# First layer's normalisation moved behind its input projection: x arrives transposed, the per-token root is applied to the products

## Chip, cores and metric

One core of a Trainium2 chip runs the whole program. The metric is the device time of one execution in microseconds (us), the median of the runs; lower is better. All tensors are float32. A matrix product in float32 is made of three passes: each operand is split into a high part in the format fp32r and a low part (what the high part leaves over), and high x high, high x low and low x high are summed in PSUM.

## What is computed

The reference is a trunk of two layers over 512 tokens and 1024 features. Cut to what the change touches:

```python
def rms_norm(x, g):
    xf = x.astype(jnp.float32)
    y = xf * lax.rsqrt(jnp.mean(xf * xf, axis=-1, keepdims=True) + NORM_EPS)
    return (y * g.astype(jnp.float32)).astype(x.dtype)

def hybrid_layer(x, w_in, w_out, g_pre, g_post, lb, g_head, sinks):
    h = rms_norm(x, g_pre)
    proj = jnp.einsum('bsd,de->bse', h, w_in)
    q_h, f_h, i_h, z_h, q_a, k_a, v_a, z_a = jnp.split(proj, SPLIT_POINTS, axis=-1)
    o_h = rms_norm(hgrn2(q_h, f_h, i_h, lb), g_head).reshape(B, S, HG_WIDTH) * jax.nn.silu(z_h)
    o_a = sliding_window_attention(rotary(q_a), rotary(k_a), v_a, sinks) * jax.nn.silu(z_a)
    y = jnp.einsum('bse,ed->bsd', jnp.concatenate([o_h, o_a], axis=-1), w_out)
    return x + rms_norm(y, g_post)
```

The root of a token (the rsqrt) is one number for a row of h. Since the projection is linear, it may be multiplied into h before the projection or into the row of proj after it. The weight g_pre belongs to a feature.

## The kernel before

**Tiling.** P = 128 partitions; the 512 tokens are NT = 4 tiles, the 1024 features KT = 8 tiles. hT (hhi and hlo, L421) holds the normalised input transposed, feature on partition: 8 feature tiles by 512 tokens. The input projection is cut into a narrow piece "kv" (keys and values, 256 columns) and 12 slabs of 512 columns: QA (attention queries, 2 slabs), IV (i, 2), FQ (forget logits and q of HGRN2, 4), ZA and ZH (the gates, 2 each). The order of the slabs is the list ORDER (L128); "kv" is first, QA second. A slab is four units of 8 steps, and a step is three matmuls of 128x512 (L293). Two units run interleaved, with three PSUM banks "pj" to take turns. For slabs with the feature on the partition (QA, FQ, ZA) the weight is the stationary operand and hT streams; for IV, ZH and kv the tokens are on the partition.

**Weights.** A weight piece (128x512) is loaded by SyncE's queue (SP) into one of 4 buffers "raw", cast to its high part whi by ScalarE (ACT, L181), and the low part wlo is made by VectorE (DVE), for odd pieces of QA by GpSimd (POOL) (L182). A load into raw waits until the piece four before it has been split. The pieces of kv are called wkv (L1013, L1014). Attention and recurrence are emitted between the steps (L968 to L975). A helper `later` runs a function after so many steps; `pin` keeps an instruction in program order on its engine, while the others are ordered by the scheduler when the program is built.

**The start (L981 to L1057).** x is loaded token by token, in tiles of 128x512 called a and x (L978), and gcol, the weight g_pre of layer 0 as 128x8, on ACT's queue. TensorE (PE) turns gcol into two banks of rows (gpre, L1005). For each token tile: ACT squares x and sums it (L383, L386), POOL takes the power -0.5 (L354, L393), DVE multiplies x by root and weight (xn, L401), PE transposes in eight pieces into PSUM (L406), ACT casts to hhi (L410) and DVE makes hlo (L414). Token tiles 1 to 3 are emitted as halves between the steps of kv. kv itself is four units, one for each token tile (24 matmuls of 128x256 each), whose result ACT copies into rkv (L448). Then comes slab QA; its results are multiplied by the tables cos_f and sin_f (tile cs) on DVE (L504 to L511). Constants are loaded and prepared during the first steps of QA.

**Results that the change touches.** IV is copied by ACT (L651). FQ: ACT takes sigmoid of a logit and of its negative from PSUM (L665, L666), or silu of q (L674). ZA: ACT takes silu from PSUM (L845), DVE multiplies by the attention output (L846). ZH: ACT takes silu (L859).

## Time and profile before

| what | value |
|---|---|
| median of 3 runs | 922.8 us (922.64 to 923.39) |
| span of the profiled execution, first to last instruction | 921.4 us |
| around the span (median less span) | 1.4 us |
| busy PE / DVE / ACT / POOL in it | 904.5 / 667.3 / 463.4 / 272.9 us |
| first matmul of slab QA in it | at 24.48 us |

A row of a timeline is: start, duration, engine, line, operation, output <- input, shape, how many merged, and in brackets the idle time of the engine before it with what ended it. "SPq" and "ACTq" are DMA issues in the queues of SyncE and ScalarE. A busy row says how long the engine was occupied in a stretch; the granted clock stands in the column PEclk (1.00 is full speed).

### The profile page before, as it was taken

The page shows a single profiled execution, that of the slowest core. Times are in us where ns is not written, and L with a number is a line of the kernel's source. Part 1 is how long each engine was busy: PE and PEld are TensorE (multiplying, and loading weights), DVE is VectorE, ACT ScalarE, POOL GpSimd, SP SyncE. Part 2 cuts the span into 40 slices and gives each one's busy share as a digit, 9 for nine tenths or more (in the row PEclk, how much of TensorE's full clock was granted, in tenths as well). Part 3 has the DMA queues.
Part 4 walks back from the last instruction along what each step waited for, and adds up shares of the span by engine and source line. Part 5 has one row for each costly group of instructions (what it writes and reads, how often), then busy time and mean ns, then how long its engine had stood idle before and what let it go on. Part 6 is the DMA issues. An engine that isn't in the chain of part 4 may idle for free.

```text
span 921.4 us, 19000 instructions
## 1 busy us (share of the span) xinstructions
PE 904.5 (98%) x7240; PEld 752.0 (82%) x7240; DVE 667.3 (72%) x1326; ACT 463.4 (50%) x1100; POOL 272.9 (30%) x292
## 2 busy tenths in 40 slices
...
GB/s 224 192 231 136 172 36 81 92 93 94 70 85 54 130 91 70 92 106 129 111 164 177 161 147 173 58 69 92 94 70 81 96 77 94 82 47 94 136 35 137
DMA packets 56570, 100.74 MB, mean 109 GB/s; under 512 B 6560, under 2 KB 9120, under 8 KB 56480
## 3 DMA queue, kind: packets, MB, share of 16 engines
...
q14 instruction: 33, 0.27, 0.1%
q10 hardware_dynamic: 288, 0.14, 0.1%
...
## 4 chain that ended last, share of the span: by engine, by line
PE 88%; DVE 6%; ACT 3%; issue 1%; POOL 1%; DMA 0%; POOLq 0%; DVEq 0%; ACTq 0%
PE pj L293 72%; PE sc L561 2%; PE sc L744 2%; PE ac L614 2%; PE ac L815 2%; DVE wlo L182 1%; PE ac L818 1%; PE ac L802 1%; PE sc L588 1%; ACT s L575 1%; PE sc L867 1%; PE sc L790 1%; POOL r L354 1%; DVE a L943 1%; PE sc L550 0%
## 5 line engine op out<-in xcount | busy, mean ns | idle before, releaser
L182 DVE TENSOR_TENSOR wlo<-raw,whi 128x512 fp32r<-128x512 f32 x249 | 182.9, 748 | 50.0 <-ACT whi L181 49.3
L181 ACT CAST whi<-raw 128x512 fp32r<-128x512 f32 x256 | 154.2, 620 | 106.0 <-PE pj L293 95.2
L293 PE MATMUL pj<-hhi,wlo 128*128 128x512 f32 x512 | 203.8, 398 | 0.0
L293 PE MATMUL pj<-hhi,whi 128*128 128x512 f32 x512 | 199.8, 390 | 0.0
L293 PE MATMUL pj<-hlo,whi 128*128 128x512 f32 x512 | 199.6, 390 | 0.0
L293 PE MATMUL pj<-whi,ops 128*128 128x512 f32 (+1 forms) x520 | 172.5, 394 | 0.0
L293 PEld LDWEIGHTS pj<-hhi,whi 128*128 128x128 f32 x512 | 96.1, 188 | 20.7
L293 PEld LDWEIGHTS pj<-whi,ops 128*128 128x128 f32 x520 | 97.2, 188 | 19.3
L293 PEld LDWEIGHTS pj<-hhi,wlo 128*128 128x128 f32 x512 | 96.1, 188 | 19.3
L293 PEld LDWEIGHTS pj<-hlo,whi 128*128 128x128 f32 x512 | 96.3, 188 | 18.6
L293 PE MATMUL pj<-whi,hlo 128*128 128x512 f32 x256 | 103.6, 405 | 0.0
L293 PE MATMUL pj<-wlo,ops 128*128 128x512 f32 (+1 forms) x260 | 100.8, 388 | 0.0
L293 PE MATMUL pj<-wlo,hhi 128*128 128x512 f32 x256 | 100.5, 392 | 0.3 <-DVE wlo L182 0.2
L293 PE MATMUL pj<-whi,hhi 128*128 128x512 f32 x256 | 100.3, 392 | 0.0
L763 POOL TENSOR_TENSOR k<-k,tot 128x256 f32<-128x256 f32 x80 | 64.2, 831 | 107.2 <-PE sc L744 57.7
L575 ACT ACTIVATE s<-sc,negm 128x128 f32<-128x128 f32 x128 | 45.5, 368 | 38.9 <-DVE negm L569 34.8
L762 DVE TENSOR_TENSOR q<-q,tot 128x256 f32<-128x256 f32 x80 | 48.8, 647 | 12.8 <-PE sc L750 7.0
L293 PEld LDWEIGHTS pj<-whi,hhi 128*128 128x128 f32 x256 | 48.1, 188 | 10.3
L293 PEld LDWEIGHTS pj<-wlo,ops 128*128 128x128 f32 x260 | 49.0, 188 | 8.8
L293 PEld LDWEIGHTS pj<-wlo,hhi 128*128 128x128 f32 x256 | 48.3, 189 | 9.1 <-DVE wlo L182 1.2
L293 PEld LDWEIGHTS pj<-whi,hlo 128*128 128x128 f32 x256 | 48.2, 188 | 8.0
L582 POOL TENSOR_TENSOR s<-s,sums 128x512 f32<-128x512 f32 x32 | 34.1, 1067 | 44.5 <-DVE sums L580 29.2
...
## 6 DMA issues: line engine op xcount, KB each, us to landing
...
```

What stands on the lines that cost most here:

```text
L181: keep(nc.scalar.copy(hi, v))
L182: keep((nc.gpsimd if i in on_pool and i % 2 else nc.vector).tensor_tensor(lo, v, hi.bitcast(F32), op=ALU.subtract))
L293: nc.tensor.matmul(u.o, lhsT=u.sta(k, u.w)[i], rhs=u.mov(k, u.w)[j], start=(n == 0), stop=(n == len(u.list) - 1))
L354: keep(nc.gpsimd.tensor_tensor(r, t, mhalf[:, 0:1], op=ALU.pow))
L561: pin(nc.tensor.matmul(S[:, h * 256:(h + 1) * 256], lhsT=q[:, 2 * hp_ + h, t_], rhs=kst[v][p][:, (n - 1) * P:(n + 1) * P], start=(h == 0 a ...
L575: nc.scalar.activation(pt[:, h * P:(h + 1) * P], cur[h], AF.Exp, bias=negm[:, h:h + 1], scale=SCALE, accum_out=sums[:, h:h + 1])
L582: nc.gpsimd.tensor_tensor(pv, pv, sums.unsqueeze(2).broadcast_to([P, 4, P]), op=ALU.mult)
L614: pin(nc.tensor.matmul(U, lhsT=vst[v][:, blk, :], rhs=d, start=(i == 0), stop=(i == len(terms) - 1)))
L744: pin(nc.tensor.matmul(L[32 * b:32 * b + 32, c:c + 16], lhsT=k[:, o_:o_ + 32], rhs=qv[:, blk:blk + qu, 1, :], start=True, stop=True, tile_ ...
L762: nc.vector.tensor_tensor(qv[:, :, 1, :], qv[:, :, 1, :], tv[:, :, 0].unsqueeze(2).broadcast_to([P, nb, hh]), op=ALU.mult)
L763: nc.gpsimd.tensor_tensor(kv_[:, :, 0, :], kv_[:, :, 0, :], tv[:, :, 1].unsqueeze(2).broadcast_to([P, nb, hh]), op=ALU.mult)
L815: pin(nc.tensor.matmul(O[:, c], lhsT=A[:, c], rhs=vs(j, n), start=(n == 0), stop=False))
```

## The change

A new input xt is x transposed on the host. Layer 0 no longer normalises and transposes:

- Eight feature tiles xs (128 features x 512 tokens) are loaded in the order in which they are needed, each pair followed by its kv weight. The first kv weight goes on ACT's queue ahead of gcol.
- hhi and hlo are x times g_pre, without the root: ACT multiplies by gcol with the cast (`high`), DVE multiplies and subtracts (`low`). The squares go another way: those of feature tiles 0, 1, 4, 5 are made elementwise on POOL, of 2, 3, 6, 7 on ACT, added up on DVE (seven adds), and summed over the partitions by four matmuls with a column of ones (total). DVE and POOL make rcol from it, the root with the token on the partition (128x4).
- The products of kv run feature tile by feature tile over all four token tiles, in two banks; the first low part of kv's weights is DVE's, the other three are POOL's.
- After two steps of QA, PE transposes rcol into a row (four transposes, rrow 128x512). The tables of QA are multiplied by it, one on DVE, one on POOL. FQ and ZA of layer 0 get one more DVE multiplication each by rrow (16 and 8 instructions of 128x512), from PSUM. kv, IV and ZH take rcol as the scale of the ACT instruction that they had.
- Constants are prepared from step 4 of QA, as before; the load of the masks waits for the four matmuls of total, whose ones lie in its buffer.

Layer 1 is not touched. The removed parts are two broadcasts of gcol and 32 transposes on PE, the scale and hlo of L401 and L414 on DVE, the squares and casts of L383, L386 and L410 on ACT, and five of POOL's small instructions.

DVE at the start of the program, before: the rows from the first root to the first two low parts of QA's weights (sc are PSUM tiles with the transposes, gcol's rows lie in PSUM as ac).

```order
L401 SCALAR_TENSOR_TENSOR xn<-a,r_140,ac_82 128x512
L401 SCALAR_TENSOR_TENSOR xn<-a,r_140,ac_81 128x512
L414 TENSOR_TENSOR hlo<-sc_79,hhi 128x4x128
L1013 CAST wkv<-raw 128x512
L414 TENSOR_TENSOR hlo<-sc_80,hhi 128x4x128
L1013 CAST wkv<-raw 128x512
L1014 TENSOR_TENSOR wkv<-raw,wkv 128x512
```

The same engine and place in the changed kernel, from the first weight cast to the first low part of QA's weights (a and b are the squares).

```order
L1032 CAST wkv<-raw 128x512
L1027 SCALAR_TENSOR_TENSOR hlo<-xs,gcol,hhi 128x512
L1035 TENSOR_TENSOR wkv<-raw,wkv 128x512
L1027 SCALAR_TENSOR_TENSOR hlo<-xs,gcol,hhi 128x512 x5
L1070 TENSOR_TENSOR a<-a 128x512 x2
L1027 SCALAR_TENSOR_TENSOR hlo<-xs,gcol,hhi 128x512 x2
L1073 TENSOR_TENSOR a<-a,b 128x512 x2
L1074 TENSOR_TENSOR a<-a 128x512
L1076 TENSOR_TENSOR a<-a,b 128x512 x2
L182 TENSOR_TENSOR wlo<-raw,whi 128x512
L1087 TENSOR_SCALAR t<-sc_79 128x4
```

All inputs of the new rows up to L182 lie in SBUF; of the old ones most have an input in PSUM. The low part of QA's first weight now stands behind all adds.

POOL at the same place, before and then in the changed kernel.

```order
L354 TENSOR_TENSOR r_140<-s_138,mhalf 128x1
L1014 TENSOR_TENSOR wkv<-raw,wkv 128x512 x2
L391 TENSOR_SCALAR s_172<-ss 128x1
L393 TENSOR_TENSOR r_174<-s_172,mhalf 128x1
L1014 TENSOR_TENSOR wkv<-raw,wkv 128x512
L354 TENSOR_TENSOR r_183<-s_181,mhalf 128x1
L391 TENSOR_SCALAR s_238<-ss 128x1
L393 TENSOR_TENSOR r_240<-s_238,mhalf 128x1
L182 TENSOR_TENSOR wlo<-raw,whi 128x512 x4
```

```order
L1054 TENSOR_TENSOR a<-xs 128x512 x2
L1035 TENSOR_TENSOR wkv<-raw,wkv 128x512 x2
L1065 TENSOR_TENSOR b<-xs 128x512 x2
L1035 TENSOR_TENSOR wkv<-raw,wkv 128x512
L182 TENSOR_TENSOR wlo<-raw,whi 128x512
L1089 TENSOR_TENSOR rcol<-t,mhalf 128x4
L182 TENSOR_TENSOR wlo<-raw,whi 128x512 x2
L1102 TENSOR_TENSOR cs<-cs,rrow 128x512
```

Up to the second large row of QA's weights POOL now has eight instructions of 128x512 in a row, six of them on x and its products; before it had three, with small ones between, and four on QA's weights later.

PE where kv ends and QA begins, changed kernel (rows of three, a step, are alike).

```order
L1041 MATMUL pj<-wkv,hhi 128x256 x4
L1083 MATMUL sc_79<-u,a 128x2 x4
L293 MATMUL pj<-hhi,wlo 128x512
L293 MATMUL pj<-hlo,whi 128x512
L293 MATMUL pj<-hhi,whi 128x512
L293 MATMUL pj<-hhi,wlo 128x512
L293 MATMUL pj<-hlo,whi 128x512
L293 MATMUL pj<-hhi,whi 128x512
L1099 MATMUL sc_80<-ident,rcol 128x128 x4
```

Behind this place PE's order is that of before, but for the transposes of the keys, which come three steps later.

The diff, cut to its core:

```diff
+        def load_tables():
+            rot.append(big.tile([P, 2, 512], F32, tag="q", name="cs", bufs=QB))
+            nc.sync.dma_start(rot[0][:, 0], cos_f)
+            nc.sync.dma_start(rot[0][:, 1], sin_f)
...
-            nc.scalar.copy(rkv[0][:, tt], o)
+            if l:
+                nc.scalar.copy(rkv[0][:, tt], o)
+            else:
+                nc.scalar.activation(rkv[0][:, tt], o, AF.Copy, scale=rcol[:, tt:tt + 1])
...
+                    if not l:
+                        nc.vector.tensor_tensor(f, o, rrow, op=ALU.mult)
+                        o = f
+                    nc.scalar.activation(k, o, AF.Sigmoid, scale=-1.0)
                     nc.scalar.activation(f, o, AF.Sigmoid)
-                    nc.scalar.activation(k, o, AF.Sigmoid, scale=-1.0)
...
+                    if not l:
+                        nc.vector.tensor_tensor(qT[h], o, rrow, op=ALU.mult)
+                        o = qT[h]
                     nc.scalar.activation(qT[h], o, AF.Silu)
...
+                if not l:
+                    nc.vector.tensor_tensor(z, o, rrow, op=ALU.mult)
+                    o = z
                 nc.scalar.activation(z, o, AF.Silu)
...
+    raws[0] = wp.tile([P, 512], F32, tag="raw", name="raw", bufs=RAW_BUFS)
+    nc.scalar.dma_start(raws[0].rearrange("p (a c) -> p a c", a=2), pieces[0])
     nc.scalar.dma_start(gcol, gcol_c)
+    state["raw"] = 1
+    for k in range(KT):
+        load_x(k)
+        if k % 2:
+            w_load(k // 2 + 2)
...
+    def first_kv(load_tables, rot, kv_evac):
+
+        warm = pj()
+        for n in (512, 256):
+            pin(nc.tensor.matmul(warm[:, 0:n], lhsT=ones[:, 0:P], rhs=ones[:, 0:n], start=True, stop=True))
+        A, V, G = nc.scalar.copy, nc.vector.tensor_tensor, nc.gpsimd.tensor_tensor
...
+        high(0)
+        whigh(0, C)
+        low(0)
+        high(1)
+        wlow(0, V)
+        low(1)
+        prod(0, ((0, 0), (1, 0), (0, 1)))
+        for c in range(2):
+            pin(G(sq[0][c], xk(c), xk(c), op=ALU.mult))
+        prod(1, ((0, 0), (1, 0), (0, 1)))
+        for j in range(1, KT // 2):
+            high(2 * j)
+            whigh(j, A)
+            low(2 * j)
+            wlow(j, G)
+            high(2 * j + 1)
+            low(2 * j + 1)
+            for c in range(2):
+                if j == 2:
+                    pin(G(sq[j][c], xk(2 * j + c), xk(2 * j + c), op=ALU.mult))
+                else:
+                    pin(nc.scalar.activation(sq[j][c], xk(2 * j + c), AF.Square))
...
+            prod(2 * j, ((0, 0), (1, 0), (0, 1)))
+            prod(2 * j + 1, ((0, 0), (1, 0), (0, 1)))
+            w_load(min(KT // 2 + j, KT // 2 + RAW_BUFS - 1))
+        load_tables()
+        total = sc()
+        for tt in range(NT):
+            pin(nc.tensor.matmul(total[:, 2 * tt:2 * tt + 2], lhsT=sq[0][0][:, tt * P:(tt + 1) * P], rhs=ones[:, 0:2], start=True, stop=True))
...
+        pin(nc.gpsimd.tensor_tensor(rcol, t, mhalf, op=ALU.pow))
...
+        def row():
+            bank = sc()
+            for tt in range(NT):
+                pin(nc.tensor.transpose(bank[:, tt * P:(tt + 1) * P], rcol[:, tt:tt + 1].broadcast_to([P, P]), ident))
+            pin(nc.scalar.copy(rrow, bank))
+            nc.vector.tensor_tensor(rot[0][:, 0], rot[0][:, 0], rrow, op=ALU.mult)
+            nc.gpsimd.tensor_tensor(rot[0][:, 1], rot[0][:, 1], rrow, op=ALU.mult)
+
+        later(2, None, row)
+        later(3, None, evacs)
+        later(4, None, constants)
```

155 lines of the change are left out of this document (64 added, 91 removed).

## The prediction

> **What bounds the kernel now.** I read the page's busy times first, then the stages, then the timeline of the start.
>
> ```profile
> PE 904.5 (98%) x7240; PEld 752.0 (82%) x7240; DVE 667.3 (72%) x1326; ACT 463.4 (50%) x1100; POOL 272.9 (30%) x292
> ```
>
> PE is busy for 98%: 17 us of the span are all that it lacks, so only PE work taken away or PE idle time filled can pay. Where is it idle at the start? A row is a stretch, its length, and PE, PEld, DVE, ACT and POOL busy.
>
> ```profile
> 0.00:5.00 5.00, 3.33 (x8) 1.78 (x9) 0.60 (x3) 2.93 (x6) 0.68 (x6) 1.00 0.56 173
> 5.00:10.00 5.00, 4.76 (x26) 3.28 (x25) 3.21 (x7) 3.36 (x6) 3.16 (x4) 1.00 1.03 354
> 10.00:15.00 5.00, 4.12 (x32) 3.65 (x31) 3.60 (x8) 3.60 (x8) 2.60 (x4) 1.00 1.00 330
> 15.00:20.00 5.00, 5.00 (x45) 4.95 (x44) 4.00 (x7) 1.75 (x5) 0.79 (x2) 1.00 0.56 175
> 25.00:30.00 5.00, 5.00 (x24) 4.13 (x23) 4.92 (x8) 2.83 (x7) 2.46 (x2) 1.00 0.67 209
> ```
>
> From 15 us on PE has no gap. The change rewrites what lies before slab QA, so its gain or loss is how much sooner or later QA's first matmul starts, plus PE work that moves behind it. Now:
>
> ```profile
> 21.51 2.18 PE L293 MATMUL pj<-wkv,hhi 128*128 128x256 f32 x16
> 23.52 1.12 PE L293 MATMUL pj<-wkv,hlo 128*128 128x256 f32 x8
> 24.48 0.40 PE L293 MATMUL pj<-hhi,wlo 128*128 128x512 f32 x1
> ```
>
> QA starts at 24.48. Matmuls of 256 columns run at 0.12 us each ((23.52 - 21.51) / 16 = 0.126, (24.48 - 23.52) / 8 = 0.12), so kv's 96 cost PE 11.5 us; the rest of the 24 us are 40 transposes, the warm-up matmuls and gaps.
>
> **The new start: first PE and ACT alone.** The 32 transposes of x and 8 of gcol go. Rows of the chain of waits price four at:
>
> ```profile
> 15.88 0.44 PE sc L406 x4
> ```
>
> 32 of them are 3.5 us. The products of kv are the same 96. ACT has 15 large instructions (8 highs, 3 casts, 4 squares); four such casts merged take 2.18 us, so 0.53 each and 8 us in all:
>
> ```profile
> 21.83 2.18 ACT L181 CAST whi<-raw 128x512 fp32r<-128x512 f32 x4
> ```
>
> The first data:
>
> ```profile
> 0.78 0.40 ACTq L981 DMA_DIRECT2D gcol<-in_gcol_dram  x1
> 3.47 0.63 ACT L386 ACTIVATE hlo<-a 128x512 fp32r<-128x512 f32 x1 [0.75 <-DMA a<-in_x_dram]
> 5.97 1.32 ACT L1013 CAST wkv<-raw 128x512 fp32r<-128x512 f32 x2 [1.06 <-DMA raw<-in_wkv_dram]
> 10.39 0.63 ACT L386 ACTIVATE hlo<-x 128x512 fp32r<-128x512 f32 x1 [0.58 <-DMA x<-in_x_dram]
> ```
>
> The first tile was in at 3.47, the ninth load of 256 KB at 10.39: (10.39 - 3.47) / 8 = 0.865 us apart. The change needs twelve (8 of x, 4 of weights); a second queue shares the engines, so I put the first x tile at 4.1, gcol, now behind 256 KB of weights, at 5.3, and the last tile at about 12.7. Neither ACT (5.4 + 8 us, with waits about 15) nor PE (6 + 11.5 = 17.5) nor the loads would hold QA beyond 18.5.
>
> **DVE and POOL: the term that decides.** DVE gets 18 large instructions up to QA's first low part: 1 cast, 8 lows, wlow, 7 adds, wlo. POOL gets 8: 4 squares, 3 kv low parts, 1 of QA. They look parallel, but the trace shows what happens where both engines work on SBUF. DVE, then POOL:
>
> ```profile
> 38.65 0.68 DVE L511 TENSOR_TENSOR rot<-pj,cs 128x512 f32<-128x512 f32 x1
> 39.25 1.41 DVE L182 TENSOR_TENSOR wlo<-raw,whi 128x512 fp32r<-128x512 f32 x1
> 40.79 1.55 DVE L521 TENSOR_TENSOR rot<-rot 128x512 fp32r<-128x512 f32 x1
> 42.27 0.68 DVE L182 TENSOR_TENSOR wlo<-raw,whi 128x512 fp32r<-128x512 f32 x1
> ```
>
> ```profile
> 38.81 1.29 POOL L514 TENSOR_TENSOR rot<-rot 128x512 f32<-128x512 f32 x1 [6.28 <-DVE rot L510]
> 40.06 1.74 POOL L515 TENSOR_TENSOR rot<-rot 128x512 f32<-128x512 f32 x1
> ```
>
> L511, with an input in PSUM, takes 0.68 beside POOL. L182 at 39.25, both inputs in SBUF, ends at 40.66, 0.56 after POOL's first instruction ended (40.10): it stood still. POOL's next took 1.74 instead of 1.29, so it waited 0.45 for DVE. Then L521 ends at 42.34, 0.54 after POOL again. They take turns: POOL 1.29, DVE 0.45, never both. A new low reads xs and hhi, an add two squares, all in SBUF: every one of the 18 is of the kind that waits.
>
> The prices, uncontended: POOL 2.52 / 2 = 1.26; DVE 0.60 from start to start (1.28 less the tail of 0.68, for a tensor by tensor), and about 0.67 for a multiply and subtract, whose duration stands in the grouped lines with 744 ns; the cast 0.42:
>
> ```profile
> 6.67 2.52 POOL L1014 TENSOR_TENSOR wkv<-raw,wkv 128x512 fp32r<-128x512 f32 x2 [0.94 <-ACT wkv L1013]
> ```
>
> ```profile
> 36.85 1.28 DVE L182 TENSOR_TENSOR wlo<-raw,whi 128x512 fp32r<-128x512 f32 x2
> 9.99 0.42 DVE L1013 CAST wkv<-raw 128x512 fp32r<-128x512 f32 x1
> ```
>
> ```profile
> L943 DVE SCALAR_TENSOR_TENSOR a<-s,r,a 128x512 f32<-128x512 f32 x7 | 5.2, 744 | 0.0
> ```
>
> The sum of turns: POOL 8 x 1.26 = 10.1; 8 DVE instructions between them at 0.45 = 3.6; the other 10 free, 0.66 on average (the last adds wait for each other, 0.74) = 6.6; together 20.3. From 4.1 that ends at 24.4, and some 0.4 is lost where POOL's turn waits for ACT's cast: **QA at 24.8**, 0.3 later than now. DVE's order adds a gap for PE inside the stage, since two adds stand ahead of lows 6 and 7. Turn by turn: POOL's fifth instruction ends at about 14.2, the others 1.74 apart (16.0, 17.7, 19.4), and behind these go low 5, an add, an add and low 6, which is thus done at 20.0, while PE is through k = 5 at 16.6 and the first four products of k = 6 at 17.2. The gap costs nothing while the adds end later still (24.1).
>
> Bounds: no other row shows a low of just this form beside POOL. From below, POOL's cheapest 128x512 (L582, 1.04: 8 x 0.22 = 1.8 less) and a start at 3.5 give 24.8 - 1.8 - 0.6 = 22.4; from above, POOL at 1.34 (8 x 0.08 = 0.6), DVE's turn at 0.56 (8 x 0.11 = 0.9) and half a us more of loads give 26.8. I take 24.8: its POOL price is from the row of the same operation and shape.
>
> ```profile
> 10.81 1.34 POOL L1014 TENSOR_TENSOR wkv<-raw,wkv 128x512 fp32r<-128x512 f32 x1
> 150.03 1.04 POOL L582 TENSOR_TENSOR s<-s,sums 128x512 f32<-128x512 f32 x1 [4.66 <-DVE sums L580]
> ```
>
> The Trainium skill (SBUF — State Buffer, "Who interferes with whom") names this: DVE and GpSimd share a port pair, an exclusive lock held for the full instruction, which a DVE instruction with two SBUF inputs needs against a GpSimd one that reads SBUF. Its "full instruction" would put 0.60 where the rows show a turn of 0.45, 1.2 more in all, and QA at 26.0; the row decides. (The trace agrees on who waits, L511 against L182.)
>
> **Behind the start.** Four transposes of rcol: 0.44, on PE's path, nothing hides them. Their input: the root of 128x4 is on POOL, whose like takes 1.01:
>
> ```profile
> L346 POOL TENSOR_TENSOR hrr<-hr,mhalf 128x4 f32<-128x4 f32 x16 | 16.2, 1013 | 1.3
> ```
>
> Total ends with QA's start, t on DVE and the root follow within 1.3, two steps of QA (6 x 0.227 = 1.36) cover them; up to 0.2 may show. Kv's banks are read by ACT once the root is there, at about 26.1, the first of the two is free by 27, and the second unit of QA, five steps in, needs it at 28.6. If it were not free, the whole of QA would wait for ACT. The table multiplications and the rotation of the keys queue on DVE at QA's start, ahead of the low parts that PE needs next. Now the third of these ends so:
>
> ```profile
> 23.52 1.43 DVE L182 TENSOR_TENSOR wlo<-raw,whi 128x512 fp32r<-128x512 f32 x1 [0.27 <-ACT whi L181]
> ```
>
> at 24.95, and PE uses it four steps in, at 27.2; later ones have more. With QA shifted by 0.3 and one DVE instruction more, 0.6, these 2.2 us cover it.
>
> The 24 multiplications by rrow cost DVE 24 x 0.673 = 16.2 us over 300 us, by L504, which reads PSUM too. The fullest stage is that of the recurrence:
>
> ```profile
> 200.00:220.00 20.00, 20.00 (x339) 16.14 (x340) 19.62 (x42) 7.28 (x14) 4.25 (x5) 1.00 0.26 70
> ```
>
> ```profile
> 216.12 0.75 DVE L762 TENSOR_TENSOR q<-q,f 128x256 f32<-128x256 f32 x2
> ```
>
> ```profile
> 219.29 1.41 PE L744 MATMUL sc<-q,k 128*32 128x16 f32 x128
> ```
>
> ```profile
> L504 DVE TENSOR_TENSOR rot<-pj,cs 128x512 f32<-128x512 f32 x4 | 2.7, 673 | 0.0
> ```
>
> L762 ends at 216.87, PE reads it at 219.29: 2.4 us cover against two or three added instructions there (1.4 to 2.0). I take 0.1; without cover it is up to 2.0. Where ACT gets the root as its scale, its instruction is the one it had: nothing.
>
> **Sum.** 0.3 + 0.44 + 0.1 + 0.1 = 0.9 (rounded): span 921.4 to 922.3, with the 1.4 around it **923.7**, against the median of 922.8. With one term of the turns at its bound at a time, QA starts between 23.0 (POOL at 1.04) and 25.7 (DVE's turn at 0.56), so the time is 922.0 to 924.7, and 925.7 with 1 us of uncovered multiplications. That is the case's own range.
>
> **Rivals.** (1) *The turns do not bind*: DVE and POOL overlap in this form. Then DVE's first low starts at about 6.0, 17 instructions of 0.66 follow (11.2), with some 1.2 of waits for ACT's highs: QA at 18.4, 6.1 earlier than now, less 0.6 behind it: 917.3. For it: rows that read PSUM do overlap, and a multiply and subtract with two SBUF inputs has no clear row beside a large POOL instruction. Against: both rows above that read two SBUF tensors waited. Half an overlap ends near 920.5.
>
> (2) *PE's clock falls in the gap* (the slow side). The place is the gap ahead of the second four products of k = 6, 17.2 to 20.0 in my schedule. The end of the program shows what a long gap does (PEclk is the third number from the end):
>
> ```profile
> 913.52 0.28 PE L293 MATMUL pj<-whi,ops 128*128 128x256 f32 x1
> ```
>
> ```profile
> 917.00:918.00 1.00, 0.00 (x0) 0.00 (x0) 1.00 (x3) 0.00 (x0) 0.00 (x0) 1.00 0.00 0
> 918.00:919.00 1.00, 0.00 (x0) 0.00 (x0) 0.20 (x1) 0.00 (x0) 0.00 (x0) 0.63 0.72 264
> 919.00:920.00 1.00, 0.00 (x0) 0.00 (x0) 0.00 (x0) 0.00 (x0) 0.00 (x0) 0.50 0.78 260
> ```
>
> After the last matmul (to 913.80) the clock stays at 1.00 until about 918.3 (0.63 is 0.26 at 1 and the rest at 0.5), then it is 0.50: it fell after 4.5 us of idleness. From a gap of 4.5 on, that is, if these products start after 21.7, the 20 that are left would take 4.8 instead of 2.4, and QA start at 21.7 + 4.8 = 26.5: 1.7 more, 925.4. For it: a late gcol, a slow POOL or each further DVE instruction before low 6 stretches the gap. Against: it needs 1.7 more than my schedule has. No row shows how long the clock stays down; if beyond QA's start, each us of that costs half a us.
>
> The Trainium skill (TensorE: Matmul & The Clock Gate, Part 1) has the fall come after one idle window of about 3.4 us, not after 4.5, and half rate until a busy window as long. By it a gap of 3.4 could do, 0.6 more than I schedule, with about 925 as the result; the trace's 4.5 lies within one to two such windows.
>
> **How the numbers follow.** My case 0.60, the likeliest, so 923.7 is the time; rival 1 with its half ways 0.20, rival 2 0.15, anything else 0.05. A measurement of this kernel tells about 0.2% from no change, 1.8 us: faster means under 921.0, slower over 924.6. Faster: rival 1 and 0.02 of the rest, 0.22. Slower: rival 2, 0.12 of my own case (its part above 924.6) and 0.01, 0.28. Same: 0.50. The range goes from 919.5, which takes in the half overlap and leaves out the full one, to 926.5, above rival 2 and a clock that stays down 2 us longer; outside are some 0.14 below and 0.05 above.
>
> **What would show it.** Right: DVE lows and adds of 1.2 us and more beside POOL, POOL instructions of 1.7 beside DVE; PE waiting for hlo ahead of k = 6 by 2 to 3 us; QA's first matmul at 24 to 26; behind it PE without gaps but for four transposes; granted clock 1.00 throughout. Wrong: lows of 0.74 while POOL runs and QA before 20 (rival 1); PEclk under 1 between 18 and 28 (rival 2); PE waiting in 200 to 220 for DVE (the cover of the 24 multiplications is gone); PE waiting for rcol; or a start that is bound by gcol, which would show as ACT idle to 6 us and beyond.

## The result: 928.9 us, 0.6% slower than before

After: 928.88 us, median of 4 runs (927.56 to 930.08); before, on the same chip: 923.1 us (922.64 to 924.32, 4 runs). The ratio is 1.0056, with a 95% interval of 1.0042 to 1.0071. The profiled execution of after has a span of 927.1 us (before 921.4), 5.7 more. The forecast was 923.7, with a range to 926.5: the kernel is slower than the whole range.

**The start came as forecast, and a little sooner.** The timeline of TensorE (PE) in after, from the products of the keys and values (L1041 is the old L293 for these) to slab QA (L293):

```profile
14.92 1.12 PE L1041 MATMUL pj<-wkv,hhi 128*128 128x256 f32 x8
18.07 0.80 PE L1041 MATMUL pj<-wkv,hlo 128*128 128x256 f32 x4 [2.04 <-DVE hlo L1027]
18.68 1.91 PE L1041 MATMUL pj<-wkv,hhi 128*128 128x256 f32 x8
23.28 1.05 PE L1083 MATMUL sc<-u,a 128*128 128x2 f32 x8 [1.06 <-DVE a L1076]
24.20 0.48 PE L293 MATMUL pj<-hhi,wlo 128*128 128x512 f32 x1
26.07 1.12 PE L1099 MATMUL sc<-ident,rcol 128*128 128x128 f32 x4
27.42 0.63 PE L293 MATMUL pj<-hlo,whi 128*128 128x512 f32 x1
```

QA starts at 24.20 (before 24.48, forecast 24.8), and PE waits ahead of k = 6 for a low part of x, as forecast. But look at the durations: eight products take 1.12 us at 14.92 and 1.91 at 18.68; a matmul of QA takes 0.48 and 0.39 to 0.40 up to 25, and 0.63 at 27.42. The same in 1-us stretches (busy PE, PEld, DVE, ACT and POOL; the third number from the end is the granted clock):

```profile
18.00:19.00 1.00, 0.93 (x6) 0.93 (x7) 1.00 (x2) 0.00 (x0) 1.00 (x1) 0.80 0.40 49
19.00:20.00 1.00, 1.00 (x7) 1.00 (x7) 1.00 (x2) 0.00 (x0) 0.16 (x1) 0.50 0.91 315
22.00:23.00 1.00, 0.22 (x2) 0.00 (x0) 0.90 (x2) 0.00 (x0) 0.00 (x0) 1.00 0.11 7
25.00:26.00 1.00, 1.00 (x4) 0.35 (x2) 0.14 (x1) 0.00 (x0) 1.00 (x2) 0.71 0.46 74
26.00:27.00 1.00, 0.99 (x6) 0.93 (x6) 0.00 (x0) 0.95 (x3) 1.00 (x2) 0.50 1.06 406
28.00:29.00 1.00, 1.00 (x5) 0.77 (x3) 1.00 (x4) 0.98 (x4) 0.00 (x0) 0.58 0.79 225
```

The clock falls to half twice: from 18.6 to about 22, and again from 25.4 to 28.8, when QA is already running. The first costs nothing (PE then waits for the sums on DVE until 23.28), the second costs time.

**Where the 5.7 us are.** All of PE's order behind the head is the same in both kernels but for the key transposes, so the same instruction can be dated in both. The first product of attention (L561, now L553) in before, in after, and in after without the 24 multiplications (experiment e2; first and last start stand behind the durations):

```profile
L561 PE MATMUL sc<-kst,qs x192: 274/283/389, 62.4 to 604.3; 128*128 128x256 f32 x192
```

```profile
L553 PE MATMUL sc<-kst,qs x192: 274/283/389, 64.5 to 610.5; 128*128 128x256 f32 x192
```

```profile
L553 PE MATMUL sc<-kst,qs x192: 274/283/386, 64.4 to 606.8; 128*128 128x256 f32 x192
```

From QA's start to there: 37.9 in before, 40.3 in after. From there to the end of the span: 859.0 in before (921.4 - 62.4), 862.6 in after, 859.3 without the multiplications. So: QA's start -0.3, the stretch behind it +2.4, the rest +3.6; together 5.7. In the rest, 3.3 go with the multiplications. PE's waits from 30 us on (in total, times, longest) name the place. After:

```profile
PE sc L553 <- ACT s L567: 3.5, 6, 0.8
PE pj L293 <- DVE q L673: 1.9, 1, 1.9
PE pj L293 <- ACT ops L851: 0.7, 1, 0.7
```

The second is a wait for a bank pj, which L673 empties; the third is one for ops, the operand that is made from z. After without the multiplications neither is there; of the three, this is left:

```profile
PE sc L553 <- ACT s L567: 3.4, 6, 0.8
```

Dated by the same PE instructions, after falls behind before at these two places: from 3.1 us at 250.6 to 5.4 at 268.1, and from 5.0 at 338.8 to 6.5 at 347.4. Without the multiplications it stays at 3.1 across the first and at 2.8 across the second.

### The profile page after: what moved, and what is told of

Same layout as the page of the kernel before. It is cut to its first block, busy times and chain, and to the rows that moved or that the text cites. A ratio compares the mean times of both kernels' runs of the same rounds, so it can differ in the third digit from the quotient of the medians.

```text
span 927.1 us, 18965 instructions
## 1 busy us (share of the span) xinstructions
PE 903.0 (97%) x7212; PEld 750.2 (81%) x7212; DVE 684.2 (74%) x1348; ACT 470.0 (51%) x1094; POOL 280.3 (30%) x292
## 4 chain that ended last, share of the span: by engine, by line
PE 77%; DVE 14%; ACT 4%; issue 3%; POOL 1%; DMA 1%; SPq 0%; DVEq 0%; POOLq 0%; ACTq 0%
PE pj L293 63%; DVE wlo L182 2%; PE sc L553 2%; PE ac L606 2%; PE ac L816 2%; PE sc L745 1%; ACT s L567 1%; DVE q L763 1%; PE ac L819 1%; PE ac L803 1%; PE sc L580 1%; DVE a L773 1%; DVE b L707 1%; PE sc L874 1%; DVE z L850 1%
## 5 line engine op out<-in xcount | busy, mean ns | idle before, releaser
L182 DVE TENSOR_TENSOR wlo<-raw,whi 128x512 fp32r<-128x512 f32 x249 | 184.2, 752 | 36.1 <-ACT whi L181 35.3
L293 PE MATMUL pj<-hhi,wlo 128*128 128x512 f32 x512 | 204.4, 399 | 0.0
L293 PE MATMUL pj<-hhi,whi 128*128 128x512 f32 x512 | 200.2, 391 | 0.0
L293 PE MATMUL pj<-hlo,whi 128*128 128x512 f32 x512 | 199.9, 390 | 0.0
L293 PE MATMUL pj<-whi,ops 128*128 128x512 f32 (+1 forms) x520 | 173.1, 395 | 2.1 <-DVE q L673 1.9
L293 PEld LDWEIGHTS pj<-whi,ops 128*128 128x128 f32 x520 | 97.2, 188 | 22.2 <-DVE q L673 2.3
L293 PEld LDWEIGHTS pj<-hhi,whi 128*128 128x128 f32 x512 | 96.3, 188 | 20.8
L293 PEld LDWEIGHTS pj<-hhi,wlo 128*128 128x128 f32 x512 | 96.4, 188 | 19.3
L293 PEld LDWEIGHTS pj<-hlo,whi 128*128 128x128 f32 x512 | 96.5, 189 | 18.5
L293 PE MATMUL pj<-whi,hlo 128*128 128x512 f32 x256 | 103.7, 406 | 0.0
L293 PE MATMUL pj<-wlo,ops 128*128 128x512 f32 (+1 forms) x260 | 100.8, 388 | 0.7 <-ACT ops L851 0.7
L293 PE MATMUL pj<-wlo,hhi 128*128 128x512 f32 x256 | 100.4, 392 | 0.3 <-DVE wlo L182 0.2
L293 PE MATMUL pj<-whi,hhi 128*128 128x512 f32 x256 | 100.3, 392 | 0.0
L567 ACT ACTIVATE s<-sc,negm 128x128 f32<-128x128 f32 x128 | 45.6, 368 | 38.3 <-DVE negm L561 38.1
L293 PEld LDWEIGHTS pj<-wlo,ops 128*128 128x128 f32 x260 | 49.0, 188 | 9.8 <-ACT ops L851 1.1
L293 PEld LDWEIGHTS pj<-whi,hhi 128*128 128x128 f32 x256 | 48.1, 188 | 10.3
L293 PEld LDWEIGHTS pj<-wlo,hhi 128*128 128x128 f32 x256 | 48.3, 189 | 8.9 <-DVE wlo L182 1.0
L293 PEld LDWEIGHTS pj<-whi,hlo 128*128 128x128 f32 x256 | 48.2, 188 | 8.1
```

Of the source, the lines that this page charges most:

```text
L182: keep((nc.gpsimd if i in on_pool and i % 2 else nc.vector).tensor_tensor(lo, v, hi.bitcast(F32), op=ALU.subtract))
L293: nc.tensor.matmul(u.o, lhsT=u.sta(k, u.w)[i], rhs=u.mov(k, u.w)[j], start=(n == 0), stop=(n == len(u.list) - 1))
L567: nc.scalar.activation(pt[:, h * P:(h + 1) * P], cur[h], AF.Exp, bias=negm[:, h:h + 1], scale=SCALE, accum_out=sums[:, h:h + 1])
```

## The experiments

Each run stands beside runs of before on its chip. The numbers, with the marks used above (QA's first matmul, attention's first product, from there to the end of the span):

| kernel | us | before there | ratio (95%) | QA | attention | rest |
|---|---|---|---|---|---|---|
| before | 923.1 | | | 24.48 | 62.4 | 859.0 |
| after | 928.88 | 923.1 | 1.0056 (1.0042 to 1.0071) | 24.20 | 64.5 | 862.6 |
| e1_fill | 929.26 | 923.59 | 1.0057 (1.0043 to 1.0070) | 25.37 | 64.3 | 863.0 |
| e15_fill_total | 928.30 | 923.18 | 1.0061 (1.0047 to 1.0074) | 24.33 | 63.2 | 862.9 |
| e3_pool_out | 926.41 | 923.59 | 1.0031 (1.0019 to 1.0044) | 22.46 | 61.4 | 862.9 |
| e5_gcol_first | 927.72 | 922.95 | 1.0057 (1.0043 to 1.0070) | 24.02 | 63.0 | 862.6 |
| e6_head | 924.76 | 922.95 | 1.0023 (1.0013 to 1.0033) | 21.17 | 61.3 | 863.9 |
| e2_no_rrow | 925.33 | 923.59 | 1.0019 (1.0010 to 1.0028) | 24.35 | 64.4 | 859.3 |
| e8_no_q | 928.06 | 922.95 | 1.0046 (1.0033 to 1.0058) | 24.62 | 65.7 | 861.2 |
| e4_act_evac | 934.83 | 923.59 | 1.0112 (1.0098 to 1.0127) | 24.61 | 65.8 | 866.9 |
| e9_prep_pool | 930.84 | 923.56 | 1.0082 (1.0068 to 1.0097) | 25.00 | 65.7 | 864.9 |
| e11_before_prep_pool | 923.83 | 923.56 | 1.0005 (0.9997 to 1.0014) | 24.54 | 62.5 | 859.0 |
| e7_kv_steps | 928.68 | 922.95 | 1.0061 (1.0048 to 1.0074) | 24.35 | 64.4 | 862.7 |
| e12_iv_plain | 928.86 | 923.56 | 1.0060 (1.0048 to 1.0073) | 24.50 | 64.6 | 862.5 |
| e10_combined | 924.36 | 923.56 | 1.0012 (1.0003 to 1.0021) | 20.69 | 59.1 | 863.4 |
| e14_head_only | 923.97 | 923.18 | 1.0012 (1.0003 to 1.0021) | 20.57 | 59.0 | 862.6 |

### The clock

**e1_fill**: keep PE busy in its gaps.

```diff
+        def fill(n):
+            for _ in range(n):
+                pin(nc.tensor.matmul(warm, lhsT=ones[:, 0:P], rhs=ones, start=True, stop=True))
...
+                if k == 6 and (i, j) == (1, 0):
+                    fill(2)
...
+        fill(3)
         total = sc()
```

> The kernel after (928.88 us) with five more matmuls on TensorE whose results nobody reads: two of 128x512 in fp32 ahead of the second four products of k = 6, three ahead of the total. Theory A (the granted clock falls in the two gaps, and what counts is the half-rate stretch behind QA's start, 25.4 to 28.8, 3.4 us of which half is lost): clock 1.00 from 8 us on, QA's first matmul still at 24.0 to 24.6 since DVE's adds set it, and 927.2 us (926.7 to 927.7). Rival (the half rate is hidden by other waits, such as the one for rcol): the clock is up and the time stays at 928.9 (within 0.5). Rival (the fill stands in PE's way): QA after 24.8 and 929.3 or more.

Two answers at once. Behind QA's start the clock stayed at 1.00, and QA to attention took 38.9 instead of 40.3. But the fill delayed QA by 1.2, so the time is that of after. What theory A said of the clock behind QA's start is confirmed in the trace (its "1.00 from 8 us on" is not: the clock was 0.50 from 8.3 to 11.7), and the third theory (the fill in PE's way) ate the gain: 929.26.

**e15_fill_total**: two fills ahead of the total alone.

```diff
+        for _ in range(2):
+            pin(nc.tensor.matmul(warm, lhsT=ones[:, 0:P], rhs=ones, start=True, stop=True))
         total = sc()
```

> The kernel after with two unread matmuls of 128x512 in fp32 ahead of the total and nothing else: in e1 the two ahead of k = 6 and the third one held QA's start up by 1.2 us, and this took back what the clock had given. Theory A: QA's start at 24.2 to 24.7 as in after, no half rate behind it, 1.2 to 2.2 less: 927.2 (926.4 to 928.0). Rival (the clock behind QA's start costs nothing): 928.9 within 0.4.

QA at 24.33, clock 1.00 behind it, 38.9 to attention: 1.4 less than in after, and the span is 926.1 instead of 927.1. The median, 928.3, lies above the 926.4 to 928.0 of theory A; it is 0.6 lower than that of after, but the ratios of the two overlap (their runs differ among themselves by 2 us). So the profile shows a price of 1.0 to 1.4 us, and the medians of few runs neither confirm nor exclude it.

In the runs that transpose the root after two steps of QA, the time from QA to attention falls in three groups: 38.9 to 39.0 with no half rate behind QA's start (e1, e3, e5, e15), 40.1 to 40.3 with one stretch of 3.4 us (after, e2, e7, e12), 40.7 to 41.2 with two (e4, e8, e9). One stretch costs 1.2 to 1.4, two 1.8 to 2.3. Where the root is transposed two steps later, so that PE does not wait for it, the time is 38.4 without half rate (e10, e14) and 40.1 with one stretch (e6): 1.7, half of 3.4. The group differs between executions of one kernel: e14's own 11 runs are seven of 923.56 to 924.15 us with a mean clock of 0.997 or 0.998 and four of 925.23 to 925.53 with 0.995 or 0.996.

**e13_gaps**: what makes the clock fall.

```diff
+    for g in range(20):
+        for i in range(8):
+            pin(nc.tensor.matmul(bank, lhsT=w[:, 0:P], rhs=w if i else c, start=True, stop=True))
+        pin(nc.vector.tensor_scalar(c, bank, 1.0 / P, None, op0=ALU.mult))
+        for _ in range(g % 5):
+            pin(nc.vector.tensor_tensor(c, c, w, op=ALU.mult))
```

> The kernel after with a tail behind the program: 20 blocks of eight matmuls (128x512 fp32, some 6.9 us at full rate), each block waiting for DVE instructions on the block before (1, 2, 3, 4 or 5 of 128x512, in turn), so TensorE idles for about 0.9, 1.5, 2.1, 2.7 and 3.3 us, four times each. Theory A1 (the clock is decided at the end of free-running stretches of 3.4 us by TensorE's share of them: it fell after shares of 25 to 40% and stayed after 47 and more): gaps up to 1.7 never lower the clock, gaps of 2.1 to 3.3 do so in some places and not in others, depending on how a stretch falls on the gap, each time for 3.4 us or a multiple. Rival A2 (it falls whenever a gap is longer than a fixed length, 4.5 us by the end of the program): no fall at all in the tail. Rival A3 (any gap from 2 us on): every gap of 2.1 and more lowers it. The time of the whole means nothing here.

The tail's gaps came out at 0.78, 1.51, 2.23, 2.96 and 3.69 us. Four of them on PE's timeline (the bracket is the gap):

```profile
942.15 1.12 PE L1156 MATMUL pj<-z,u 128*128 128x512 f32 x2 [1.51 <-DVE z L1159]
951.52 2.06 PE L1156 MATMUL pj<-z,u 128*128 128x512 f32 x2 [2.23 <-DVE z L1159]
963.31 1.12 PE L1156 MATMUL pj<-z,u 128*128 128x512 f32 x2 [2.96 <-DVE z L1159]
1013.54 2.07 PE L1156 MATMUL pj<-z,u 128*128 128x512 f32 x2 [2.96 <-DVE z L1159]
```

Two matmuls behind a gap take 1.12 at full and 2.06 at half rate: after 2.23 us the clock was down, and the same gap of 2.96 left it up at 963 and down at 1013.

```profile
965.00:966.00 1.00, 1.00 (x4) 1.00 0.00 0
1014.00:1015.00 1.00, 1.00 (x2) 0.50 0.00 0
```

Over all of them: 0.78 and 1.51 never lowered it (0 of 8), 2.23 always (4 of 4), 2.96 in 2 of 4, 3.69 in 3 of 3. The falls behind these gaps, dated from the 1-us stretches, are at 951.56, 975.46, 1002.76, 1013.00, 1026.66, 1053.96, 1074.44, 1105.16 and 1115.40: each distance is a multiple of 3.413 us to within 0.02. So there is a fixed grid, and what counts is PE's busy share of a grid stretch: it fell after shares of 26 to 40%, and not after 42% (ahead of 1064.2), 56 and 57% (around 961.8; there the gap of 2.96 lies half in each of two stretches). The same holds in after: 15.18 to 18.59 has 1.37 us of products, 40%. It stayed low for 3.4 us where the next stretch was busy, and for 6.8 where that stretch had only 54 or 73% (from 1074.44 and 1115.40). A1 holds; a fixed length (A2) and "every gap from 2 us" (A3) do not.

Two things go beyond e13. The border is not sharp: on the same grid in the other profiles the clock fell after 43% (e1, ahead of 8.25), 45% (e4, ahead of 344.60), 48% (e15, ahead of 8.53) and 49% (e9, ahead of 343.92), and stayed after 48 and 49% (e1, ahead of 257.42; e15, ahead of 257.71). And small matmuls hardly count: after's second fall, at 25.42, follows a stretch that is 69% busy, but 42% without total's matmuls of 128x2; in e2 and e7 it is 52 to 54% with them and 26 to 28% without. Nor do they bring the clock back: in e8 and e9 it stayed low behind stretches that were 94 to 100% busy with them, and 43 to 64% without. Stretches with 53% (e13, 968.63 to 972.05) and 59% (after, 254.12 to 257.53) of other matmuls left the clock up.

The Trainium skill (TensorE: Matmul & The Clock Gate, Part 1) has a free-running window of 4096 cycles at 1.2 GHz, 3413 ns, for this. The grid of 3.413 agrees with it to the digit; its "after ≥1 idle window" is too mild for these traces, since a stretch that was 40% busy was idle enough.

### The turns of DVE and POOL in the head

The turns themselves stand in after's timeline, POOL above and DVE below; each DVE instruction alone would take 0.6 to 0.67 and each POOL one 1.0 to 1.3:

```profile
12.86 2.94 POOL L1065 TENSOR_TENSOR b<-xs 128x512 f32<-128x512 f32 x2
15.77 1.71 POOL L1035 TENSOR_TENSOR wkv<-raw,wkv 128x512 fp32r<-128x512 f32 x1
```

```profile
13.38 2.97 DVE L1070 TENSOR_TENSOR a<-a 128x512 f32<-128x512 f32 x2
16.27 3.43 DVE L1027 SCALAR_TENSOR_TENSOR hlo<-xs,gcol,hhi 128x512 fp32r<-128x512 f32 x2
```

**e3_pool_out**: three more instructions on DVE, four on ACT, none of these seven on POOL.

```diff
-            pin(G(sq[0][c], xk(c), xk(c), op=ALU.mult))
+            pin(nc.scalar.activation(sq[0][c], xk(c), AF.Square))
...
-            wlow(j, G)
+            wlow(j, V)
...
-                if j == 2:
-                    pin(G(sq[j][c], xk(2 * j + c), xk(2 * j + c), op=ALU.mult))
-                else:
-                    pin(nc.scalar.activation(sq[j][c], xk(2 * j + c), AF.Square))
+                pin(nc.scalar.activation(sq[j][c], xk(2 * j + c), AF.Square))
```

> The kernel after with POOL taken out of the head: its four squares go to ACT, its three low parts of the kv weights to DVE, so DVE has 21 instructions of two SBUF inputs instead of 18 and POOL only QA's first low part. Theory C (DVE and POOL take turns, and that sets QA's start): DVE's run at 0.6 to 0.67 each, the adds end some 14 us after the first low at 6, and QA starts at 20 to 21.5 instead of 24.2: 925.7 us (924.5 to 926.8; a clock that falls in another place can cost or save up to 1.7 of it). Rival (turns do not set it; the number of instructions on ACT and DVE does): ACT gets 2.4 us and DVE 2.0 us more, QA at 24 to 26, 929 to 931 us.

More work on DVE, and QA starts 1.7 sooner, at 22.46 (expected 20 to 21.5). The time, 926.41 us, is in theory C's range, but not by the start alone: in the profiled execution 1.7 are the start and 1.4 the clock, which did not fall behind QA (38.9 to attention). DVE's timeline in e3:

```profile
15.65 0.68 DVE L1035 TENSOR_TENSOR wkv<-raw,wkv 128x512 fp32r<-128x512 f32 x1
16.25 0.74 DVE L1027 SCALAR_TENSOR_TENSOR hlo<-xs,gcol,hhi 128x512 fp32r<-128x512 f32 x1
16.91 1.28 DVE L1070 TENSOR_TENSOR a<-a,b 128x512 f32<-128x512 f32 x2
18.23 1.67 DVE L1071 TENSOR_TENSOR a<-a 128x512 f32<-128x512 f32 x1
```

Everything now goes at its own pace but L1071, which meets the one instruction left on POOL (QA's low part, 17.90 to 19.36) and takes 1.67 instead of 0.69.

**e5_gcol_first**: 4 KB ahead of 256 KB on ACT's queue.

```diff
+    nc.scalar.dma_start(gcol, gcol_c)
     nc.scalar.dma_start(raws[0].rearrange("p (a c) -> p a c", a=2), pieces[0])
-    nc.scalar.dma_start(gcol, gcol_c)
```

> The kernel after with its two first loads on ACT's queue exchanged: gcol (4 KB) ahead of the 256 KB of kv weights, so that ACT's first high part does not wait until 5.46. Theory C (the turns of DVE and POOL set QA's start, from the first low part on): the run of turns begins up to 1 us sooner and QA's first matmul comes at 23.2 to 23.7 instead of 24.2: 928.2 us (927.4 to 928.9). Rival (POOL's turns begin with the x tiles at 3.84 and the weights' arrival, so the start of the low parts does not matter): QA at 24.2, 928.9.

QA at 24.02: DVE's first low part started at 5.92 instead of 6.22, but its later ones then waited for POOL and ACT, so 0.2 is left of it. The ratio is that of after (the median is in theory C's range, but before measured less on this chip too). The rival holds.

**e6_head**: e3, e5's edit, and

```diff
-        for n in (512, 256):
+        for n in (512, 512, 128):
...
+        pin(nc.tensor.matmul(warm, lhsT=ones[:, 0:P], rhs=ones, start=True, stop=True))
         total = sc()
...
-        later(2, None, row)
         later(3, None, evacs)
+        later(4, None, row)
```

> The kernel of e3 (POOL out of the head) with four more edits of the head: gcol loaded first, a longer warm-up on TensorE (512, 512 and 128 columns in fp32 instead of 512 and 256) so that it has no gap before the first product, one unread matmul of 512 columns ahead of the total, and the transposes of the per-token root two steps later. Theory: products at full rate from the first, QA at 20.5 to 21.7 (e3: 22.46), no wait for rcol, so 1 to 1.7 us under e3 (926.4): 925.0 (924.4 to 925.7). Rival (the run of adds on DVE is bound by the last x tile and by ACT, not by its start): QA at 22.2 or later, 926.0 to 926.6.

QA at 21.17 and 924.76 us, as expected. In the profiled execution (927.35 us, the slowest of its eight) one fill was not enough: the clock was down from 22.5 to 25.9. Its rest, 863.9, is 1.3 more than in after. The wait behind q (2.1) explains 0.2 of that; behind it the clock fell once more, for one stretch, since the one before was 38% busy:

```profile
254.62:258.04 3.42, 3.42 (x8) 2.74 (x9) 3.35 (x11) 1.98 (x4) 0.00 (x0) 0.50 0.35 77
```

Half of 3.4 us is 1.7, enough for what is left. So a wait in the middle of the program can cost its length and a stretch at half rate on top.

### The 24 multiplications by rrow

**e2_no_rrow**: the lines with `op=ALU.mult` by rrow left out for f, q and z.

```diff
-                    if not l:
-                        nc.vector.tensor_tensor(f, o, rrow, op=ALU.mult)
-                        o = f
...
-                    if not l:
-                        nc.vector.tensor_tensor(qT[h], o, rrow, op=ALU.mult)
-                        o = qT[h]
...
-                if not l:
-                    nc.vector.tensor_tensor(z, o, rrow, op=ALU.mult)
-                    o = z
```

> The kernel after without the 24 multiplications by rrow in layer 0's f, q and z features (these keep no per-token root; all else is computed). The head is the same. Theory B (these instructions fill DVE where it empties PSUM banks, so PE waits 1.9 us at 256 behind q, 0.9 at 333 to 342 behind z, and some 0.5 in smaller places): about 3 us less, 925.8 (925.3 to 926.6), with no PE wait for DVE or ops between 200 and 400. Rival (PE's waits there come from the shifted start or from the scheduler's order and would stay): 928.9 (within 0.6).

925.33 us, 0.37% under after by the ratios (3.4 us), and the rest of the program takes 859.3, 0.3 from before's 859.0. Theory B holds, and the size is 3.3 us, not 0.1.

How 0.68 us on an engine that is 74% busy costs 3.3: the largest wait. DVE in after:

```profile
254.40 1.42 DVE L763 TENSOR_TENSOR q<-q,tot 128x256 f32<-128x256 f32 x4
256.69 0.69 DVE L715 TENSOR_TENSOR q<-b,f 128x512 f32<-128x512 f32 x1 [0.53 <-ACT b L708]
257.29 0.68 DVE L673 TENSOR_TENSOR q<-pj,rrow 128x512 f32<-128x512 f32 x1
```

PE then, behind 1.92 us of idleness, and before's counterpart on ACT:

```profile
258.03 0.50 PE L293 MATMUL pj<-whi,ops 128*128 128x512 f32 x1 [1.92 <-DVE q L673]
```

```profile
251.15 0.60 ACT L674 ACTIVATE q<-pj 128x512 f32<-128x512 f32 x1
```

L673 empties a bank pj that PE needs. In before ACT emptied it, as the first step on q; now it stands in DVE's queue behind a piece of the recurrence and behind L715, which itself waits for ACT. Further up DVE has no idle time in after, where before has some: after, then before, DVE being the third busy time.

```profile
210.00:220.00 10.00, 9.87 (x226) 7.90 (x225) 10.00 (x18) 3.03 (x5) 4.12 (x4) 1.00 0.31 86
220.00:230.00 10.00, 10.00 (x167) 8.23 (x166) 10.00 (x26) 3.75 (x6) 4.10 (x4) 1.00 0.35 103
```

```profile
210.00:220.00 10.00, 10.00 (x235) 8.07 (x236) 9.62 (x20) 4.50 (x8) 4.25 (x5) 1.00 0.16 34
220.00:230.00 10.00, 10.00 (x241) 8.31 (x229) 8.26 (x17) 2.14 (x4) 5.51 (x6) 1.00 0.39 129
```

That this backlog is what makes DVE late at 256 is argued, not shown. DVE was not full all the way: ahead of L707 at 242.18 it stood idle for 2.58 us, until ACT had worked on the f that DVE had multiplied at 237.39.

**e8_no_q**: q's 8 multiplications left out (the second hunk of e2).

> The kernel after without the 8 multiplications by rrow of layer 0's q features (q keeps no per-token root); f and z keep theirs. Theory B (the largest wait, 1.9 us at 256, belongs to the bank that q's second multiplication empties): 927.0 us (926.5 to 927.5), and the waits behind z at 333 to 342 stay at about 0.9. Rival (DVE is too full in 245 to 260 whichever of the instructions goes, so the wait stays or moves to f): over 928.

The wait of 1.9 is gone, the one behind z (0.9) is not, and the rest takes 861.2, 1.4 less than in after. The time, 928.06, fell by 0.8 only and lies above what was expected: the profiled execution lost two stretches to half rate at the head, 0.8 more than after's (41.1 from QA to attention instead of 40.3). Of the five executions two had a mean clock of 0.998 and took 925.7 and 926.05 us, three had 0.993 to 0.995 and took 928.06 to 928.59. B holds for the place; f and z carry the other 1.9.

**e4_act_evac**: ACT empties the bank, DVE multiplies in SBUF.

```diff
-                        nc.vector.tensor_tensor(f, o, rrow, op=ALU.mult)
+                        nc.scalar.copy(f, o)
+                        nc.vector.tensor_tensor(f, f, rrow, op=ALU.mult)
```

and the same for q and z.

> The kernel after with f, q and z of layer 0 copied out of PSUM by ACT (24 more ACT instructions of 0.6), and multiplied by rrow on DVE in SBUF. Theory B1 (what PE waits for is the PSUM bank that is held until DVE, behind its queue, has read it): the wait of 1.9 at 256 goes, and the time falls by 1.5 to 2.8, to 926.1 to 927.4. Rival B2 (DVE has too much work there, whoever empties the bank; and from SBUF the multiplication also waits for POOL): PE waits for what DVE makes later instead, 928.9 to 931.

934.83 us; the rest takes 4.3 more than in after. PE's wait moves to ACT (first row: in total, times, longest), and ACT's timeline shows why:

```profile
PE pj L293 <- ACT q L674: 2.9, 1, 2.9
```

```profile
255.34 0.63 ACT L677 ACTIVATE q<-q 128x512 f32<-128x512 f32 x1 [2.69 <-DVE q L675]
255.88 3.40 ACT L780 COPY a<-sc 32x64 f32<-32x64 f32 x16
259.75 0.58 ACT L674 COPY q<-pj 128x512 f32<-128x512 f32 x1
```

B1's gain did not come, and the loss goes beyond B2's range too. The copy that frees the bank (L674) stands behind silu of the head before, which waits 2.69 for DVE's multiplication, and behind 16 small copies. It is still the bank that PE waits for, but it is now freed by a queue that itself waits for DVE. A second wait, 1.6 for ops, was followed by a stretch at half rate (344.6 to 348.0), which is part of the 4.3.

**e9_prep_pool** and **e11_before_prep_pool**: two instructions of each head's preparation to POOL, in after and in before.

```diff
+                eng = nc.vector if l else nc.gpsimd
-                nc.vector.tensor_tensor(q2, qb2, f2[:, :, 0].unsqueeze(2).broadcast_to([P, SEQ // 2, 2]), op=ALU.mult)
-                nc.vector.tensor_tensor(f2[:, :, 0], f2[:, :, 0], f2[:, :, 1], op=ALU.mult)
+                eng.tensor_tensor(q2, qb2, f2[:, :, 0].unsqueeze(2).broadcast_to([P, SEQ // 2, 2]), op=ALU.mult)
+                eng.tensor_tensor(f2[:, :, 0], f2[:, :, 0], f2[:, :, 1], op=ALU.mult)
```

> The kernel after with two of DVE's instructions per head of layer 0's preparation (q times f over 128x512, f times f over 128x256; 16 in all, about 9 us of DVE) on POOL, which is 30% busy. The 24 multiplications by rrow stay. Theory B (DVE is full from 200 to 260, so PSUM banks are emptied late): the wait of 1.9 at 256 falls below 0.8, and the time by 1 to 2, to 926.9 to 927.9. Rival (POOL's instructions make DVE wait in turn, or come too late for the next stage): no gain or a loss, 928.7 to 931.

> The kernel before with the edit of e9 alone, so that a gain of e9 or e10 isn't put down to the new start when it would help the old one as much. Theory B (in before, ACT empties those banks and DVE is full nowhere that counts): no change, 923.0 within 0.6. Rival: POOL's longer instructions delay the preparation, 924 or more.

The wait behind q shrank as theory B had it, but the time rose to 930.84 and the rest to 864.9 (2.3 more than in after). The wait for ops, which is made from z, grew from 0.7 to 2.0:

```profile
PE pj L293 <- ACT ops L852: 2.0, 2, 1.8
PE pj L293 <- DVE q L673: 0.6, 1, 0.6
```

These two changes cancel (1.3 each). What is left is largely the clock, which in this execution fell behind the longer wait for one stretch; half of it is 1.7:

```profile
343.92:347.33 3.41, 3.41 (x10) 2.62 (x9) 1.63 (x4) 0.00 (x0) 0.00 (x0) 0.50 0.00 0
```

In before the same edit cost nothing measurable (1.0005, 0.9997 to 1.0014). So 9 us taken from DVE by way of POOL don't help: the relief at the bank came back at ops. Nor does e9 show that a full DVE in 200 to 230 makes the bank late: one of the two instructions that it moves is L715 itself, which stood right ahead of L673 with a wait of 0.53 and 0.6 of work, and these alone are most of the 1.3.

### The 0.8 us between 62 and 195

The first spread of the recurrence (L688, now L689) starts at 195.5 in before and 198.5 in after and at 198.4 in e2: 133.1 behind attention's first product against 134.0. PE waits once more for the exponentials (L567, six times instead of five). The place, in after and in before (L571 is the old L579; L592 the old L600):

```profile
86.16 1.10 DVE L571 TENSOR_TENSOR sums<-sums,es 128x4 f32<-128x4 f32 x1 [1.06 <-ACT es L570]
```

```profile
86.16 1.09 POOL L592 TENSOR_SCALAR_AFFINE_SELECT pprev<-a 128x1024 fp32r<-128x1024 f32 x1
```

```profile
84.06 0.16 DVE L579 TENSOR_TENSOR sums<-sums,es 128x4 f32<-128x4 f32 x1 [1.05 <-ACT es L578]
```

```profile
84.06 1.12 POOL L600 TENSOR_SCALAR_AFFINE_SELECT pprev<-a 128x1024 fp32r<-128x1024 f32 x1
```

In both kernels the two start in the same 10 ns; in before DVE goes first and needs 0.16, in after it stands for the whole of POOL's instruction, 1.10, and the chain behind it is 0.9 late. It is no accident of one execution: DVE takes 1.10 at this place in the profiles of all runs with the new head, wherever its start lies, and 0.16 in the two with the old head (before and e11).

**e7_kv_steps**: PE's order as in before (keys rotated at step 9 and transposed at 21 instead of 12 and 24).

```diff
-                later(12 if l == 0 else 8, None, kv_rotate)
-                later(24 if l == 0 else 16, ("k", l, 0), kv_store)
+                later(9 if l == 0 else 8, None, kv_rotate)
+                later(21 if l == 0 else 16, ("k", l, 0), kv_store)
```

> The kernel after with the rotation of the keys at step 9 instead of 12 and their transposes at step 21 instead of 24, so that all of TensorE's order after the head's is that of before. Question: the 0.8 us that every run with the new head, also the one without the multiplications, loses between 62 and 195 us. Theory D (it comes from the order, since the keys are transposed three steps later): the wait of 0.69 at 91 goes, 928.1 us (927.6 to 928.5). Rival (it is a chance meeting of a DVE instruction with a POOL one there, or the longer scaled copies on ACT): 928.9 within 0.4, the wait stays or moves.

No change (1.0061 against 1.0056), the wait stays: theory D falls.

**e12_iv_plain**: iv copied without its scale.

```diff
-                if l:
-                    nc.scalar.copy(t, o)
-                else:
-                    nc.scalar.activation(t, o, AF.Copy, scale=rcol[:, tt:tt + 1])
+                nc.scalar.copy(t, o)
```

> The kernel after with layer 0's values (the iv slabs) copied out of PSUM without the per-token root as ACT's scale (that root is left out of them). Question: the 0.8 between 62 and 195 us. Theory E (the scaled copy takes 0.69 instead of 0.59; the exponentials behind it come 0.1 later, and a DVE instruction of 128x4 at 86.16 loses its turn to a POOL instruction of 1.1, which before it won by that much): the wait of 0.69 at 91 goes and the time is 928.1 (927.7 to 928.5). Rival (another cause): the wait stays, 928.9 within 0.4.

No change either; with the copy back at 0.59 the two still meet (86.25 both) and DVE still loses. Theory E falls. What tips a tie of 10 ns stays open, and with it why the new head always loses it; that this meeting is the 0.8 rests on the four rows above, and no run took it away in the new kernel.

### All together

**e10_combined** is e6 with two fills, QA's low parts on DVE (`on_pool.discard` for layer 0 too) and e9's edit; **e14_head_only** is e10 without e9's edit.

> All edits that shorten something, together: the head of e6 with two unread matmuls instead of one ahead of the total and QA's first low parts all on DVE, and the two instructions of e9 on POOL. Against e6 (924.8 us): the head 0.4 sooner, no half rate behind QA's start (1.2), and 1 to 2 from e9: 922.0 to 922.8, against 923 of before: equal to it or faster by up to 0.1%. If e9's rival holds: 923 to 925.

> The kernel of e10 without e9's edit, so the new head alone: gcol first, POOL out of the head, the longer warm-up, two unread matmuls ahead of the total, the transposes of the root two steps later. All 24 multiplications as in after. Theory (e10's 59.1 at attention's first product, and 862.6 from there on as in after): span 921.7, time 923.4 (922.8 to 924.2), 0.05% over before within the interval. Rival (e9's edit was a gain in e10, by the shorter wait at 256): 925 or more.

```profile
20.57 0.48 PE L293 MATMUL pj<-hhi,wlo 128*128 128x512 f32 x1
23.38 0.60 PE L1098 MATMUL sc<-ident,rcol 128*128 128x128 f32 x4
```

QA starts 3.9 sooner than in before, the root's transposes wait for nothing, attention starts 3.4 sooner (59.0 against 62.4), and the rest gives back 3.6: span 921.6 against 921.4. e10 and e14 both measure 1.0012 (1.0003 to 1.0021). e10's 924.36 misses its 922.0 to 922.8 and lies where e9's rival put it: e9's edit adds 0.8 to the rest (863.4), so it is a loss there too. e14's median, 923.97, is in its range (to 924.2). No version beat before. A head that is worth 3.4 us and multiplications that cost 3.3 cancel.

## Why the prediction was wrong

**QA's start: the mechanism right, the number partly by luck.** 24.8 was forecast from turns of DVE and POOL, 24.20 came, and e3 shows by taking POOL out that the turns delay the start (by 1.7). But the sum of turns held only as a whole. POOL's first two squares took 1.04 each where 1.26 was put (the row of the same shape; the lower bound named 1.04), and only its last four instructions were held up by DVE, not all eight. In return POOL stood idle for 2.50 and 1.44 us until ACT had cast the second and third kv weight, where 0.4 was put. Two squares between DVE's turns took 2.94, so a turn of DVE was 2.94 / 2 - 1.04 = 0.43 (0.45 put). The Trainium skill's lock for the full instruction (SBUF — State Buffer, "Who interferes with whom"), by which QA would have come at 26.0, is not borne out in its length. Rival 1 (turns that don't bind, 917.3) is out. gcol came where it was put (ACT waited for it to 5.46; forecast 5.3), and e5 shows that it did not bind.

**The clock, put at nothing: wrong, by 1.4.** The gap ahead of k = 6 was where the forecast had it, shorter (2.04 against 2.8), and it did "cost nothing", although the clock fell behind it. The fall that cost came behind the next stretch, with the wait ahead of total, which the forecast did not ask about. The step that failed is the threshold: "it fell after 4.5 us of idleness", read off the end of the program, and from there "it needs 1.7 more than my schedule has". At the end of the program 4.5 was one reading of a rule with a phase: the last grid stretch with work in it was still more than half busy, and only the next, empty one lowered the clock. e13 shows the rule. A gap of 2.04 and one of 1.06 with eight tiny matmuls behind it were enough, and the half rate lasted to 28.8, 4.6 us past QA's start. So rival 2's mechanism came, without the delay of the products that its price was made of; its side remark, that each us of low clock beyond QA's start costs half a us, is the part that came true (one stretch of 3.4: 1.2 to 1.4 where PE also waits for rcol, 1.7 in e6).

**Behind the start: 0.54 forecast without the multiplications, 1.0 measured** (QA to attention 38.9 to 39.0 with the clock up, against 37.9). The four transposes are 0.4, as forecast. Their wait for rcol is 0.4, not 0.1: the root on POOL took 1.41 instead of 1.01, beside a DVE instruction with two SBUF inputs. With the transposes two steps later (e14) QA to attention is 38.4. The other 0.2 is not placed.

**The multiplications: wrong, and the largest error; 0.1 forecast, 2.0 as the bound, 3.3 measured** (e2). The failed step: "2.4 us cover it against two or three added instructions". That cover was read between one DVE instruction and its reader on PE in 200 to 220. But the new instructions also took over from ACT the emptying of PSUM banks, and a bank is freed when DVE's queue gets there: around 256 that cost 2.3 us. And for z they stand at the head of the chain that makes ops: around 340 that cost 1.5. (Of these 3.8 some 0.5 comes back further on.) The row of 200 to 220 had DVE at 19.62 of 20, that is, no slack to take 1.4 to 2.0 in; that this is why DVE is late at 256 fits the rows but was not shown by a run of its own. The list of what would prove the step wrong named the engine but not the place: it looked for PE waiting for DVE in 200 to 220, and the waits came at 256 and 340. The bound was too low because it was made from one place of a chain that has several.

**What wasn't forecast: 0.8** in attention, read as a lost tie between DVE and POOL (no run shows it), and 0.5 that layer 1 gives back (its cause stays open).

Sum: -0.3 + 1.0 + 1.4 + 3.3 + 0.8 - 0.5 = 5.7.
